# Retention's sample states handled four sequences at a time: column groups, 32-row pairs and 1 MB transfers

## The chip, the cores and the metric

The kernel runs on one core of a Trainium2 chip. The metric is the device time of one launch in microseconds; a change is judged by the median of several runs. Names of engines: TensorE (PE, and PEld for its weight loads), VectorE (DVE), ScalarE (ACT), GpSimd (POOL) and SyncE (SP). Transfers are issued by SyncE and GpSimd here and carried by 16 DMA engines.

## The reference, cut to what matters

One step of a hybrid encoder layer over 1024 prompt positions and 8 sample sequences of 16 positions each. The change touches the retention branch for the samples. Each of the 8 sequences has, for each of 4 heads, a state of 256 x 512 numbers that is read, used for the output and updated:

```python
def _retention_block(q, k, v, s, log_g):
    ...
    scores = jnp.einsum('bhnd,bhmd->bhnm', q, k) * decay
    out = jnp.einsum('bhnm,bhmv->bhnv', scores, v)
    q_dec = jnp.exp(lg * (idx + 1.0)).astype(dt)
    out = out + jnp.einsum('bhnd,bhdv->bhnv', q * q_dec[None, :, :, None], s)
    k_dec = jnp.exp(lg * (L - 1.0 - idx)).astype(dt)
    s_new = jnp.exp(log_g * L).astype(dt)[None, :, None, None] * s + jnp.einsum(
        'bhmd,bhmv->bhdv', k * k_dec[None, :, :, None], v)
    return out, s_new
```

The third-last einsum is called the state product below (q times the old state), the last one the update (k times v, added to the decayed state). Everything is in float32.

## The kernel before

Positions are cut into nine tiles of 128 (tile 0 holds the 8 x 16 sample positions, tiles 1 to 8 the prompt), and the tiles into three groups; group 0 is tiles 0 and 1. Each group goes through the trunk: `retention`, `gating`, `project`, `query`. After the trunk, or beside it, a product-key retrieval runs: its top-k work, gathered expert rows (GpSimd issues the gathers), and a long dense stage at the end.

Weights come in units of 512 KB, loaded by SyncE's queue up to 13 units ahead in group 0 (`load`, `take`). Each unit is split into two float32r parts, a high one on ScalarE (`whi`, L200) and a low one on VectorE (`wlo`, L204), and a product is made of three matmuls (`products`). The weight products are L176 (`gemm_f`) and L192 (`gemm_t`).

Only group 0 has sample states. For each head `retention` makes q, k and v, then `score`, then for tile 0 the loop over 8 sequences `b` and 2 halves `c` of the 256 state rows, 16 steps a head, 64 in all. This is called the state stretch of a head; it stands between the matmul of L383, with which tile 0's output `po` begins, and the two of L406 for tile 1. A step loads a state half of 128 x 512 (`load_state`, L292, 256 KB, ten buffers, four steps ahead), masks k to the 16 rows of sequence `b` and splits it (`kb`, L202 on ScalarE and L206 on VectorE), multiplies the masked `kb` with `vs` in three 128-row float32r matmuls (L395, the update), multiplies `qm` with the old state in float32 (L397, the state product; it writes 32 rows of `po`, which is one group of 32 columns of the array, given by `r = 2 * LS * (b // 2)`), adds the update on VectorE (L398) and stores the state half (L399, from GpSimd's queue). `qm` holds q of sequence `b` in 32 columns of which 16 are zero, so two sequences (`b` even and odd) add into the same 32 rows.

PSUM tiles named `sps` have four buffers, shared by `po`, the updates `pu` and the scores. A fp32 matmul has two records on TensorE, a float32r matmul one.

A scheduler sets the order of the instructions on every engine from the order in the code, priorities and its own costs; so weight products of the next gemm (L192) stand between the steps. On each engine the order is fixed at run time.

Of the kernel before, what the change touches and what calls it, by code (L numbers as in the profile page):

```python
# [8 lines left out]
F32 = mybir.dt.float32  # L9
# [5 lines left out]
OP = mybir.AluOpType  # L15
AX = mybir.AxisListType

P = 128
# [3 lines left out]
HEADS, DK, DV = 4, 256, 512  # L22
PH, NKEYS, TOPK = 8, 128, 16
HK = PH * TOPK
NB, LS = 8, 16
PAST = 512
EPS = 1e-6
GAMMA = [1.0 - 2.0 ** (-5.0 - h) for h in range(HEADS)]
# [7 lines left out]
K_KDP, K_EPP, K_DMP, K_TRI, K_IOTA, K_ID = 0, 4, 8, 520, 648, 776  # L36
N_CST = 904

S_KDS, S_EPS, S_DMS, S_TRS = 0, 32, 36, 548
N_SMP = 676  # L40

GROUPS = [[0, 1], [2, 3, 4, 5], [6, 7, 8]]

# [11 lines left out]
def step_kernel(ctx: ExitStack, tc: tile.TileContext, x, state, wall, wst, bs, rows, vec, cst, smp, cosd, sind, euv,  # L55
                eud, evd,
                y_p, y_s, st_p, st_s, sgu_s):
    nc = tc.nc
# [7 lines left out]
    sp = trunk_ps.enter_context(tc.tile_pool(name="sp", bufs=4, space=bass.MemoryType.PSUM))  # L66
# [76 lines left out]
    def products(w, a):  # L143
        return [(w[0], a[0]), (w[1], a[0]), (w[0], a[1])]
# [126 lines left out]
                yield from query(gi, pl, tl, nt, T, tT, rs, unit)  # L271
                flush(True)

    NSB, SBA = 10, 4

    def retention(pl, tl, nt, T, sample, hT, pb):
        cosT = pl.tile([P, T], F32, name="cosT")
# [2 lines left out]
        nc.sync.dma_start(sinT, sind[:, tl[0] * P:tl[0] * P + T])  # L280
        cos2 = cosT[:, None, :].to_broadcast([P, 2, T])
        sin2 = sinT[:, None, :].to_broadcast([P, 2, T])
        if sample:
            cm = pl.tile([P, S_TRS], F32, name="cm")
            nc.sync.dma_start(cm, smp[:, :S_TRS])
            Sbs = {}

            def load_state(n):
                for m in range(n if n > SBA - 1 else 0, min(n + 1, HEADS * NB * 2)):
                    Sbs[m] = pl.tile([P, DV], F32, name="Sb", bufs=NSB)  # L290
                    j, c = divmod(m, 2)
                    nc.sync.dma_start(Sbs[m], state[j % NB, j // NB, c * P:(c + 1) * P])  # L292

            load_state(SBA - 1)
            qm = pl.tile([P, 2, NB, 2 * LS], F32, name="qm")
            nc.vector.memset(qm, 0.0)

# [37 lines left out]
        for h in range(HEADS):  # L335
# [3 lines left out]
            q = rotary(ps, "q")  # L339
# [37 lines left out]
            for i, t in enumerate(tl):  # L377
# [4 lines left out]
                if t == 0:  # L382
                    mm(po, sc, v[:, i], start=True, stop=False)  # L383
                    vs = [pl.tile([P, DV], F32R, name=f"vs{j}") for j in range(2)]
                    split(vs, v[:, i])
                    for b in range(NB):
                        c0 = S_KDS + h * NB + b
                        for c in range(2):
                            load_state(2 * (h * NB + b) + c + SBA)
                            Sb = Sbs.pop(2 * (h * NB + b) + c)  # L390
                            kb = [pl.tile([P, P], F32R, name=f"kb{j}", bufs=2) for j in range(2)]
                            split(kb, kt[:, c * P:(c + 1) * P], cm[:, c0:c0 + 1])
                            pu = sp.tile([P, DV], F32, name="sps")
                            for j, (x, y) in enumerate(products(kb, vs)):
                                mm(pu, x, y, start=j == 0, stop=j == 2)  # L395
                            r = 2 * LS * (b // 2)
                            mm(po[r:r + 2 * LS], qm[:, c, b], Sb, start=False, stop=b % 2 == 1 and c == 1)  # L397
                            nc.vector.scalar_tensor_tensor(Sb, Sb, GAMMA[h] ** LS, pu, op0=OP.mult, op1=OP.add)  # L398
                            nc.gpsimd.dma_start(st_s[b, h, c * P:(c + 1) * P], Sb)  # L399
                        yield 3.5  # L400
                else:
                    mm(po, sc, v[:, i], start=True, stop=S is None)
                    pus = []
# [652 lines left out]
def constants():  # L1056
# [6 lines left out]
    for h in range(HEADS):  # L1063
        g = GAMMA[h]
        c[:, K_KDP + h] = g ** (P - 1 - m) / 16
        c[:, K_EPP + h] = EPS / g ** (2 * (m + 1))
        c[:, K_DMP + h * P:K_DMP + (h + 1) * P] = np.where(tri, g ** (-(m[:, None] + 1)) / 16, 0)
        for b in range(NB):
            d[:, S_KDS + h * NB + b] = np.where(m // LS == b, g ** (LS - 1 - m % LS) / 16, 0)
        d[:, S_EPS + h] = EPS / g ** (2 * (m % LS + 1))  # L1070
        d[:, S_DMS + h * P:S_DMS + (h + 1) * P] = np.where(tri & same, g ** (-(m[:, None] % LS + 1)) / 16, 0)
    c[:, K_TRI:K_TRI + P] = tri
# [55 lines left out]
```

## Time and profile before

| | before |
|---|---|
| median of 3 runs (lowest to highest) | 3954.83 us (3950.23 to 3957.91) |
| the profiled execution's own time | 3949.41 us |
| its span in the profile | 3947.5 us |
| TensorE busy, share of the span | 92% |
| VectorE, ScalarE, GpSimd | 87%, 47%, 26% |
| mean rate of HBM traffic over the span | 297 GB/s |

The span is the time from the first to the last instruction in the trace; the launch's own time has 1.9 us around it. Busy times are shares of the whole span, so an engine with a high share can still be idle in the stretch that a change touches. TensorE's matmuls are pipelined and the ends of their records are modelled: what a matmul costs is read from the distance between starts, which the pieces of the chain of waits give, not from the length of a record.

### The profile page before, as it was taken

How to read it: one execution, taken by the hardware profiler on the slowest of the kernel's cores; microseconds unless marked ns; L12 is line 12 of the kernel's file. 1: busy time of each engine (PE TensorE's matmuls, PEld its weight loads, DVE VectorE, ACT ScalarE, POOL GpSimd, SP SyncE). 2: the span in 40 equal slices, each digit the busy share in tenths (PEclk: the TensorE clock that was granted, in tenths of full speed). 3: DMA queues.
4: the chain of work that ended last, by engine and by line, in shares of the span. 5: the costliest groups of instructions: out<-in, count | busy, mean ns of one | idle time of the engine just before them, and what ended most of it. 6: DMA issues, size and time to landing. Idle time of an engine off the chain costs nothing.

```text
span 3947.5 us, 54950 instructions
## 1 busy us (share of the span) xinstructions
PE 3636.9 (92%) x19724; PEld 3085.6 (78%) x19724; DVE 3450.0 (87%) x6439; ACT 1847.1 (47%) x3879; POOL 1022.0 (26%) x740
## 2 busy tenths in 40 slices
PE   8999999999999898889889846999899999999998
PEld 6769988788788777778889845777777777777776
DVE  5555699999989799889898888999899999999996
ACT  4435544444343443765656737334334344443443
POOL 0010002333334230121212221234223333333330
PEclk9999999999999899999999967999999999999999
DMA  8665637999989893685777884899779999999994
GB/s 292 216 211 190 206 117 281 358 353 345 352 330 364 344 332 119 212 288 197 264 264 278 308 302 134 343 382 379 287 289 375 381 362 388 369 388 372 377 382 187
DMA packets 245298, 1176.03 MB, mean 298 GB/s; under 512 B 28193, under 2 KB 45345, under 8 KB 161057
## 3 DMA queue, kind: packets, MB, share of 16 engines
q0 software_dynamic: 105984, 721.47, 49.0%
q1 hardware_dynamic: 139040, 451.06, 31.2%
q8 instruction: 155, 2.54, 0.3%
q14 instruction: 119, 0.97, 0.1%
HBM read 1095.87 MB, written 76.55 MB: 297 GB/s over the span
## 4 chain that ended last, share of the span: by engine, by line
issue 34%; PE 19%; POOL 16%; DVE 16%; DMA 11%; ACT 3%; POOLq 0%; SPq 0%; DVEq 0%; ACTq 0%
POOL gat L778 16%; PE gps L176 6%; DMA pdr<-st 4%; PE gps L192 4%; DMA gat<-in_euv_dram,idx 3%; DVE acc L749 2%; PE S L1001 2%; DVE wlo L204 2%; DVE gat L739 2%; PE res L972 2%; PE sps L397 1%; PE sps L395 1%; DMA s<-ssp 1%; ACT st L806 1%; DVE ktmp L633 1%
## 5 line engine op out<-in xcount | busy, mean ns | idle before, releaser
L778 POOL DMA_INDIRECT gat<-in_euv_dram,idx x640 | 948.2, 1482 | 2378.8 <-DVE acc L749 1639.5
L739 DVE CUSTOM_DVE_ANT_0 gat<-gat,tx 128x1024 f32<-128x1024 f32 x640 | 782.6, 1223 | 68.7 <-DMA gat<-in_euv_dram,idx 52.7
L749 DVE SCALAR_TENSOR_TENSOR acc<-gat,sdot,acc 128x1024 f32<-128x1024 f32 x640 | 821.4, 1283 | 1.3 <-ACT sdot L745 0.9
L972 PE MATMUL res<-ev,g 128*128 128x512 f32 x2304 | 802.4, 393 | 8.8 <-ACT g L200 8.6
L1001 PE MATMUL S<-h,whi 128*128 128x512 f32 x2048 | 758.8, 398 | 10.0 <-ACT a L1006 5.9
L192 PE MATMUL gps<-whi,h 128*128 128x256 f32 x3456 | 661.2, 290 | 5.8 <-DVE rot L302 2.2
L204 DVE TENSOR_TENSOR wlo<-wraw,whi 128x1024 fp32r<-128x1024 f32 x428 | 523.7, 1224 | 82.1 <-ACT whi L200 80.7
L192 PEld LDWEIGHTS gps<-whi,h 128*128 128x128 f32 x3456 | 556.4, 196 | 29.5 <-issue 22.2
L200 ACT CAST whi<-wraw 128x1024 fp32r<-128x1024 f32 x428 | 447.3, 1045 | 260.6 <-PE gps L176 143.2
L744 ACT ACTIVATE sdot<-sdot 128x1 f32<-128x1 f32 x640 | 128.3, 202 | 839.4 <-DVE sdot L739 837.8
L972 PEld LDWEIGHTS res<-ev,g 128*128 128x128 f32 x2304 | 433.2, 189 | 111.5 <-ACT g L200 17.9
L192 PE MATMUL gps<-wlo,h 128*128 128x256 f32 x1728 | 500.8, 290 | 19.7 <-DVE wlo L204 19.7
L176 PE MATMUL gps<-h,whi 128*128 128x256 f32 (+2 forms) x1920 | 499.4, 343 | 10.5 <-ACT pb L328 5.8
L1001 PEld LDWEIGHTS S<-h,whi 128*128 128x128 f32 x2048 | 388.2, 190 | 118.6 <-ACT a L1006 33.3
L176 PE MATMUL gps<-y,whi 128*128 128x256 f32 (+2 forms) x1536 | 404.7, 346 | 21.1 <-ACT y L202 9.1
L1001 PE MATMUL S<-h,wlo 128*128 128x512 f32 x1024 | 402.0, 393 | 0.0
L176 PEld LDWEIGHTS gps<-h,whi 128*128 128x128 f32 x1920 | 345.0, 193 | 37.0 <-ACT pb L328 6.0
L192 PEld LDWEIGHTS gps<-wlo,h 128*128 128x128 f32 x1728 | 338.3, 196 | 34.0 <-DVE wlo L204 21.4
L176 PE MATMUL gps<-h,wlo 128*128 128x256 f32 (+2 forms) x960 | 328.5, 342 | 7.8 <-DVE wlo L204 7.7
L176 PEld LDWEIGHTS gps<-y,whi 128*128 128x128 f32 x1536 | 276.1, 193 | 47.3 <-ACT y L202 9.8
L200 ACT CAST ev<-wraw 128x512 fp32r<-128x512 f32 x256 | 158.1, 622 | 260.5 <-PE res L972 129.1
L176 PE MATMUL gps<-y,wlo 128*128 128x256 f32 (+2 forms) x768 | 263.1, 343 | 2.2 <-DVE wlo L204 2.2
(216 smaller groups left out, 5297.1 us busy)
## 6 DMA issues: line engine op xcount, KB each, us to landing
wraw<-in_wall_dram SPq DMA_DIRECT2D x300, 512.0 KB
wraw<-in_eud_dram SPq DMA_DIRECT2D x128, 512.0 KB
wraw<-in_evd_dram SPq DMA_DIRECT2D x128, 512.0 KB
gat<-in_wall_dram SPq DMA_DIRECT2D x84, 512.0 KB
pdr<-st POOLq DMA_DIRECT2D x32, 1024.0 KB
pt<-pdr SPq DMA_DIRECT2D x16, 2048.0 KB
Sb<-in_state_dram SPq DMA_DIRECT2D x64, 256.0 KB
out_dram<-Sb POOLq DMA_DIRECT2D x64, 256.0 KB
```

The source lines that it names most:

```text
L176: mm(ps[:, c, :T], x, y, start=kh == 0 and k == 0 and j == 0, stop=kh == nk - 1 and k == 3 and j == len(pr) - 1)
L192: mm(ps[:, i], y, x, start=kh == 0 and k == 0 and j == 0 and i % 2 == 0, stop=kh == 1 and k == 3 and j == len(pr) - 1 and last)
L200: nc.scalar.copy(parts[0], src)
L204: nc.vector.tensor_tensor(parts[1], src, parts[0].bitcast(F32), op=OP.subtract)
L395: mm(pu, x, y, start=j == 0, stop=j == 2)
L397: mm(po[r:r + 2 * LS], qm[:, c, b], Sb, start=False, stop=b % 2 == 1 and c == 1)
L739: nc.vector.tensor_tensor_reduce(out=b[:, :D], in0=b[:, :D], in1=d["x"], op0=OP.mult, op1=OP.add, scale=1.0, scalar=0.0, accum_out=d["s"][ ...
L744: nc.scalar.activation(d["s"][:, j:j + 1], d["s"][:, j:j + 1], AF.Gelu_apprx_tanh)
L749: nc.vector.scalar_tensor_tensor(d["acc"], b[:, D:], d["s"][:, j:j + 1], d["acc"], op0=OP.mult, op1=OP.add)
L778: nc.gpsimd.indirect_dma_start(out=b, out_offset=None, in_=euv, in_offset=bass.IndirectOffsetOnAxis(ap=d["idx"][:, j:j + 1], axis=0))
L972: mm(ps, x, y, start=start and i == 0, stop=stop and i == 2)
L1001: mm(ps, x, y, start=k == 0 and i == 0, stop=k == KD - 1 and i == 2)
```

## The change

Four sequences of the same parity (`a` is 0 or 1, `q` is 0 to 3, `b = 2 * q + a`) are taken together, so a head has four steps `(a, c)` instead of 16.

- One load of 1 MB brings the state halves of four sequences (`four`, L294, three buffers, one step ahead in the code); one store takes them back (L412).
- k is masked and split once a step: the mask now keeps every second block of 16 rows, so that each block of 32 rows holds one sequence of the step.
- The state products of the four sequences stand one after another in the code; they write four different groups of 32 rows of `po` (L400).
- The updates (L406) multiply only the 32 rows of a sequence, and two sequences take turns in each of the three matmuls of a product: rows 0 to 31 and 32 to 63, then 64 to 95 and 96 to 127. `keep_in_program_order` holds that order, except for the first matmul of a pair.
- VectorE still adds each update to its state by itself (L410). The yields sum to the same, 28 a head.

```diff
-S_KDS, S_EPS, S_DMS, S_TRS = 0, 32, 36, 548
-N_SMP = 676
+S_KDS, S_EPS, S_DMS, S_TRS = 0, 8, 12, 524
+N_SMP = 652
...
-    NSB, SBA = 10, 4
...
+        def four(z, h, a, c):
+            return z.rearrange("(q a) h k v -> a h k q v", a=2)[a, h, c * P:(c + 1) * P]
+
...
             def load_state(n):
-                for m in range(n if n > SBA - 1 else 0, min(n + 1, HEADS * NB * 2)):
-                    Sbs[m] = pl.tile([P, DV], F32, name="Sb", bufs=NSB)
-                    j, c = divmod(m, 2)
-                    nc.sync.dma_start(Sbs[m], state[j % NB, j // NB, c * P:(c + 1) * P])
-
-            load_state(SBA - 1)
+                if n < HEADS * 4:
+                    h, a, c = n // 4, n // 2 % 2, n % 2
+                    Sbs[n] = pl.tile([P, 4, DV], F32, name="Sb", bufs=3)
+                    nc.sync.dma_start(Sbs[n], four(state, h, a, c))
+
+            load_state(0)
...
-                    for b in range(NB):
-                        c0 = S_KDS + h * NB + b
+
+
+                    for a in range(2):
+                        c0 = S_KDS + h * 2 + a
                         for c in range(2):
-                            load_state(2 * (h * NB + b) + c + SBA)
-                            Sb = Sbs.pop(2 * (h * NB + b) + c)
+                            n = (h * 2 + a) * 2 + c
+                            load_state(n + 1)
+                            Sq = Sbs.pop(n)
                             kb = [pl.tile([P, P], F32R, name=f"kb{j}", bufs=2) for j in range(2)]
                             split(kb, kt[:, c * P:(c + 1) * P], cm[:, c0:c0 + 1])
-                            pu = sp.tile([P, DV], F32, name="sps")
-                            for j, (x, y) in enumerate(products(kb, vs)):
-                                mm(pu, x, y, start=j == 0, stop=j == 2)
-                            r = 2 * LS * (b // 2)
-                            mm(po[r:r + 2 * LS], qm[:, c, b], Sb, start=False, stop=b % 2 == 1 and c == 1)
-                            nc.vector.scalar_tensor_tensor(Sb, Sb, GAMMA[h] ** LS, pu, op0=OP.mult, op1=OP.add)
-                            nc.gpsimd.dma_start(st_s[b, h, c * P:(c + 1) * P], Sb)
-                        yield 3.5
+                            for q in range(4):
+                                r = slice(2 * LS * q, 2 * LS * (q + 1))
+                                mm(po[r], qm[:, c, 2 * q + a], Sq[:, q], start=False, stop=a == 1 and c == 1)
+                            for qs in ((0, 1), (2, 3)):
+                                pu = {q: sp.tile([P, DV], F32, name="sps") for q in qs}
+                                for j, (x, y) in enumerate(products(kb, vs)):
+                                    for q in qs:
+                                        r = slice(2 * LS * q, 2 * LS * (q + 1))
+                                        ins = mm(pu[q], x[r], y[r], start=j == 0, stop=j == 2)
+                                        if (j, q) != (0, qs[0]):
+                                            tc.keep_in_program_order(ins)
+                                for q in qs:
+                                    nc.vector.scalar_tensor_tensor(Sq[:, q], Sq[:, q], GAMMA[h] ** LS, pu[q],
+                                                                   op0=OP.mult, op1=OP.add)
+                            nc.gpsimd.dma_start(four(st_s, h, a, c), Sq)
+                            yield 7.0
...
-        for b in range(NB):
-            d[:, S_KDS + h * NB + b] = np.where(m // LS == b, g ** (LS - 1 - m % LS) / 16, 0)
+        for b in range(2):
+            d[:, S_KDS + h * 2 + b] = np.where(m // LS % 2 == b, g ** (LS - 1 - m % LS) / 16, 0)
```

TensorE's order before, in head 1's state stretch: from the sixth state product (L397) on, with updates (L395) and weight products (L192) between. A trailing x4 is four such instructions in a row.

```order
L397 MATMUL sps<-Sb,qm 32x512
L395 MATMUL sps<-vs_1169,kb_1253 128x512
L397 MATMUL sps<-Sb,qm 32x512 x4
L192 MATMUL gps<-whi,h_133 128x256
L395 MATMUL sps<-vs_1169,kb_1254 128x512
L395 MATMUL sps<-vs_1170,kb_1253 128x512
L395 MATMUL sps<-vs_1169,kb_1266 128x512
L397 MATMUL sps<-Sb,qm 32x512
L192 MATMUL gps<-wlo,h_133 128x256
L192 MATMUL gps<-whi,h_134 128x256
L192 MATMUL gps<-whi,h_133 128x256
```

Here the products mostly stand alone between updates, with one row of four.

TensorE's order in the changed kernel at the start of the same stretch, from its first matmul on (L385 is the former L383, L400 the products, L406 the updates).

```order
L385 MATMUL sps<-v,sc 128x512
L400 MATMUL sps<-Sb,qm 32x512 x4
L406 MATMUL sps<-vs_1079,kb_1085 128x512 x3
L406 MATMUL sps<-vs_1079,kb_1086 128x512 x2
L406 MATMUL sps<-vs_1080,kb_1085 128x512 x2
L400 MATMUL sps<-Sb,qm 32x512
L406 MATMUL sps<-vs_1079,kb_1085 128x512
L406 MATMUL sps<-vs_1079,kb_1086 128x512 x2
L406 MATMUL sps<-vs_1080,kb_1085 128x512 x2
L400 MATMUL sps<-Sb,qm 32x512 x3
L406 MATMUL sps<-vs_1079,kb_1116 128x512
L400 MATMUL sps<-Sb,qm 32x512
```

The products have moved together: the first step's four stand in a row, the second step's are one and three, the third step's too, and the last step's are four again further down. The updates of a pair take turns.

SyncE's queue in the changed kernel, from head 1's state stretch on: state loads (L294), weight loads (L124) and a store of the prompt's state (L157).

```order
L294 DMA Sb<-in_state_dram 128x4x512 x2
L124 DMA wraw<-in_wall_dram 128x1024
L294 DMA Sb<-in_state_dram 128x4x512
L157 DMA stsp_114<-S 128x1024
L294 DMA Sb<-in_state_dram 128x4x512
L124 DMA gat<-in_wall_dram 128x1024 x2
```

Thirteen, one and two loads of 256 KB stood in these places before; now it is two, one and one of 1 MB, of which the first is for the last step of head 1 and the other three for head 2.

From the gating stage of group 0 to the end of the program the order on every engine is the same in both kernels, and 48 loads, 48 stores and 48 pairs of mask-and-split are fewer ahead of it.

## Rows read from the trace of the kernel before

**Rows 1.** The page: the span, and busy time of each engine.

```profile
span 3947.5 us, 54950 instructions
...
PE 3636.9 (92%) x19724; PEld 3085.6 (78%) x19724; DVE 3450.0 (87%) x6439; ACT 1847.1 (47%) x3879; POOL 1022.0 (26%) x740
```

**Rows 2.** Windows by stretch: heads 0 to 3's state stretches and what lies between.

```profile
core 0: us, PE busy (x) PEld busy (x) DVE busy (x) ACT busy (x) POOL busy (x), PEclk, DMA share, GB/s
43.16:78.52 35.36, 35.36 (x107) 13.74 (x106) 18.12 (x37) 9.09 (x24) 8.89 (x16) 1.00 0.88 299
...
113.34:148.37 35.03, 35.03 (x122) 15.86 (x122) 18.61 (x38) 11.20 (x26) 8.52 (x16) 1.00 0.67 226
148.37:192.58 44.21, 44.21 (x374) 44.19 (x373) 25.41 (x35) 23.12 (x30) 0.12 (x1) 1.00 0.62 206
192.58:227.61 35.03, 35.03 (x122) 15.85 (x122) 18.61 (x38) 11.20 (x26) 8.53 (x16) 1.00 0.71 234
...
271.82:306.85 35.03, 35.03 (x123) 15.85 (x122) 18.62 (x38) 11.21 (x26) 8.52 (x16) 1.00 0.51 174
```

**Rows 3.** Chain of waits, head 1's state stretch: start us, us, what.

```profile
by line: PE sps L397 38.7%; PE sps L395 36.6%; PE gps L192 14.7%; PE sps L406 4.9%; PE sps L383 2.6%; PE sps L402 2.4%
...
113.34 0.91 PE sps L383 x2
...
124.33 0.97 PE sps L397 x2
...
125.73 1.85 PE sps L397 x8
...
131.87 0.93 PE sps L395 x4
...
145.28 0.86 PE sps L402 x2
...
146.65 1.72 PE sps L406 x4
```

**Rows 4.** Chain of waits, a run of weight products ahead of head 1's stretch.

```profile
100.49 11.52 PE gps L192 x96
```

**Rows 5.** Timeline of TensorE's weight loads: a lone product, then the row of four.

```profile
59.72 0.14 PEld L397 LDWEIGHTS sps<-Sb,qm 128*32 128x32 f32 x2 [0.36 <-issue]
...
125.66 0.15 PEld L397 LDWEIGHTS sps<-Sb,qm 128*32 128x32 f32 x4 [0.24 <-issue]
126.11 0.12 PEld L397 LDWEIGHTS sps<-Sb,qm 128*32 128x32 f32 x2 [0.31 <-issue]
126.54 0.12 PEld L397 LDWEIGHTS sps<-Sb,qm 128*32 128x32 f32 x2 [0.31 <-issue]
127.50 0.19 PEld L192 LDWEIGHTS gps<-whi,h 128*128 128x128 f32 x1 [0.84 <-issue]
```

**Rows 6.** Groups by line in head 1's stretch: busy us, mean ns | idle before.

```profile
L398 DVE SCALAR_TENSOR_TENSOR Sb<-Sb,sps 128x512 f32<-128x512 f32 x16 | 10.6, 685 | 16.1 <-PE sps L395 13.8 <-PE sps L397 2.3
...
L395 PEld LDWEIGHTS sps<-vs,kb 128*128 128x128 f32 x48 | 8.3, 188 | 7.1 <-ACT kb L202 4.0 <-DVE kb L206 2.3
L202 ACT ACTIVATE kb<-kt,cm 128x128 fp32r<-128x128 f32 x16 | 6.3, 401 | 17.2 <-PE sps L395 16.5 <-DVE Sb L398 0.6
...
L206 DVE SCALAR_TENSOR_TENSOR kb<-kt,cm,kb 128x128 fp32r<-128x128 f32 x16 | 5.1, 346 | 0.2 <-ACT kb L202 0.2
...
L397 PEld LDWEIGHTS sps<-Sb,qm 128*32 128x32 f32 x32 | 2.0, 108 | 4.8 <-issue 4.6
```

**Rows 7.** Timelines of GpSimd's stores and SyncE's queue, heads 0 and 1.

```profile
118.31 0.54 POOL L399 DMA_DIRECT2D out_dram<-Sb  x1 [39.95 <-DVE kb L206]
...
40.73 28.57 SPq L292 DMA_DIRECT2D Sb<-in_state_dram  x16
...
120.65 26.89 SPq L292 DMA_DIRECT2D Sb<-in_state_dram  x13
```

**Rows 8.** GpSimd's issue of a 1 MB store, later stage: ns min/median/max.

```profile
L808 POOL DMA_DIRECT2D pdr<-st x32: 1152/1213/1317, 1583.8 to 2455.7; - x32
```

## Prediction

> **What bounds the kernel now.** I began with the page: a span of 3947.5 us with TensorE at 92% [rows 1], and no other engine above VectorE's 87%. That share is a mean over stages, so I cut the stage of the change, group 0's retention, into stretches: in every one of them TensorE is busy from end to end at a granted clock of 1.00 (2.4 GHz), while VectorE has work for about half of a state stretch, ScalarE for a third and GpSimd for a quarter [rows 2]. So TensorE's queue sets the length here, and a microsecond taken off ScalarE, VectorE or an issuing queue alone is worth nothing.
>
> Next the chain of waits through head 1's state stretch, 113.34 to 148.37 us. All of its pieces are TensorE's: 38.7% products (L397) and 36.6% updates (L395) [rows 3]. Heads 2 and 3 show the same busy times [rows 2]. After it the chain stays on TensorE's weight products, and the order of instructions on every engine is the same in both programs from the gating stage on; so what retention saves moves everything behind it forward, one for one.
>
> **Prices on TensorE.** A full-width weight product takes 11.52 / 96 = 0.12 us [rows 4]. An update takes 0.93 / 4 = 0.23; a lone state product 0.97 (two records of one fp32 matmul); L383, L402 and the two of L406 take 0.91, 0.86 and 1.72, so 3.49 together [rows 3]. The 35.03 us of the stretch are then 3.49, 32 weight products (3.8), 48 updates (11.0), and 16.7 for 16 products: twelve lone ones at 0.97 and one row of four, which took 1.85 [rows 3], are 13.5. The 3.2 left over I put down to changing the array's shape: 13 times in and out, 0.125 a change. One shows at 127.50: the weight loader stood idle for 0.84 before it took the next full-width weights, where otherwise it runs ahead [rows 5].
>
> **The row of four** is what decides. It holds the seventh to tenth product of the head (b = 3, 3, 4, 4), so its products 1 and 2 write column group 1, products 3 and 4 group 2. Their first weight loads, four of them, all begin inside 0.15 us at 125.66, and two further pairs follow at 126.11 and 126.54 [rows 5]: one product of either group ran beside one of the other, so four took 1.85 where lone ones take 3.9. TensorE reached past product 2 to start product 3. In the new program four in a row have four different groups.
>
> **The sum, heads 1 to 3.** Unchanged: 3.49. The new order puts 39 weight products inside the stretch, 32 before: 4.7 (and 0.84 fewer behind it, so the old stretch on this footing is 35.9). The 16 products stand in six rows (4, 1, 3, 1, 3, 4). All groups of a row at once is 6 x 0.97 = 5.8; two at once, 4 x 1.85 + 2 x 0.97 = 9.3. I take 5.8, since the second group cost nothing that the rows show; 9.3 stays as a bound. The 48 updates are as many as before, but on 32 rows each, in pairs on two row groups and two PSUM tiles. No row of this kernel has a 32-row matmul. Below: 24 x 0.23 = 5.5, side by side as the column groups were. Above: one after another, 11.0; with the weight load of 0.188 [rows 6] no longer hidden, 20.1. I take 5.5, as the nearest rows show two groups of the array truly side by side [rows 5]. Changes of shape: the new order has 22, 2.75. Sum 22.3. Then waits: a pair needs two of the three PSUM tiles that the output leaves free, so it waits for an update of 0.69 on VectorE [rows 6]; the weight products set between the pairs cover most of that. I add 1.5 for this and the loads: 23.8. Saved: 35.9 - 23.8 = 12.1 a head.
>
> **Head 0.** 35.36 before [rows 2] with 16 weight products; the new order has 55, so 40.0 on the same footing. New: 3.49 + 6.6 + four rows of four at 0.97 (3.9) + 5.5 + 21 changes (2.6) = 22.1, and 2.5 for waits, since its loads after the first are issued only from about 41 us on, behind weights [rows 7]: 24.6. Saved: 15.4. Together 15.4 + 3 x 12.1 = 52; I forecast 51.
>
> **What I cost at nothing.** 48 of 64 mask-and-split pairs go: 48 x 0.40 on ScalarE and 48 x 0.35 on VectorE [rows 6], 36 us of work under a TensorE that is never idle. Of VectorE's 18.6 us in a stretch [rows 2] 12 splits go, and 14.5 stay beside TensorE's 24. SyncE issues 16 loads instead of 64; GpSimd issues 4 stores a head in place of 16, and a 1 MB store elsewhere in the kernel costs it 1.21 [rows 8], with nothing else to do there. If TensorE's cover were gone, VectorE would hold a head at 14.5 and no lower.
>
> **Loads.** Three tiles of 1 MB, so step 3's load waits for step 0's store. Before, a 256 KB store issued at 118.31 freed its tile for the load at 120.65, 2.34 us later [rows 7]. The DMA engines moved 299 GB/s at 88% busy [rows 2], about 340 when full, so 0.79 MB more is 2.3: 4.6 for the store, and as much for the load. Step 0's updates end some 7 us into the stretch (0.91, two rows of products, twelve updates in pairs, five changes, two sums of 0.69 and the 0.6 or so that GpSimd starts behind them); 7 + 4.6 + 4.6 = 16.2. TensorE wants the tile where 16.4 of the 22.3 are done. That is just in time, and contention is in the 1.5. SyncE's queue holds weight loads behind these waiting loads, as before: in head 1 it issued 13 state loads over 26.89 us [rows 7], and no TensorE wait followed, since up to 13 units are fetched ahead. Head 1 moves 226 GB/s x 35.0 + 206 x 44.2 = 17 MB [rows 2]; in 67 us instead of 79 that is 254 GB/s, below 340.
>
> **Where the skill bears.** The Trainium skill, page "TensorE: Matmul & The Clock Gate", section Part 3, says that weight loads overlap running matmuls only where the row group differs, which would deny it to column groups. This case's trace differs: at 126.11 two loads of 0.12 begin while both groups stream [rows 5]. The same page measured four 32-row tiles at 3.07 times one; an estimate from that (77% efficiency, so 1.53 for a pair) makes the updates 7.2 instead of 5.5 a head and the saving 45 in all; no run here shows it yet.
>
> **The rivals.** Updates do not pair (13%): 11.0 for 5.5, and VectorE's wait vanishes under them: 36 saved, 3919.
>
> Products go two at once (10%): 9.3 for 5.8, and 7.4 for 3.9 in head 0: 38 saved, 3917. With unpaired updates too (6%): 31.3 and 31.2 a head, 23 saved, 3932.
>
> Weight loads are laid bare within a row (4%): 32 loads of 0.108 [rows 6], 3.5 a head, 14 less: 3918. The overlap at 126.11 speaks against it. This is where the Trainium skill's rule (TensorE: Matmul & The Clock Gate, Part 3) would lead.
>
> The load of step 3 comes late (6%): if a 1 MB turn takes four of the old 2.07 (26.89 / 13), 8.3 each way, it lands at 24 instead of 16.2: 7 a head, 28 less, 3932. Against it: those turns were paced by the updates, not by the engines.
>
> Nothing (4%): if a 32-row update costs 0.40, the 48 of them eat what the products give.
>
> Slower (5%): each 32-row update is its own change of shape, with load bare: 0.23 + 0.19 + 0.125 = 0.54, 26.1 a head. Then 42.8 stands against 35.9 (and 42.7 against 40.0): 23 us slower, 3978. It decides from 0.40 on. Speaking for it: no row shows what a new row group costs; against it: a second column group cost next to nothing, as its two loads fit with the first two into 0.15 us, where those of a lone product take 0.14 [rows 5].
>
> **How the numbers follow.** The profiled execution took 3949.4, 5.4 below the median of 3954.8 that is to be predicted; from the median, 3954.8 - 51 = 3904. That case has 52%. Without any wait the saving is 17.9 + 3 x 13.6 = 59, so 3896, and the runs differ by some 4: low 3892. The high end takes in both half-gains together: 3935. A measurement of this kernel tells 0.2%, 8 us, from no change: faster 0.91, same 0.04, slower 0.05.
>
> **What will show it.** Right: rows of L400 with eight matmul records in about 1.0 us instead of 1.85; pairs of L406 that start within 0.02 us of each other; state stretches of 22 to 25 us from L385 to the last L419; everything from the gating stage on shifted by one amount. Wrong: L406 at 0.23 or more apart within a pair; a wait of TensorE on a load at the last L400 row of a head; TensorE waiting for VectorE's L410 for more than 2 us a head; or a granted clock below 1.00 in the stretches.

## The result, and the profile after

The changed kernel took 3911.4 us (median of 4 runs, 3908.6 to 3916.1) against 3954.9 us for the kernel before on the same chip: a ratio of 0.9892, 95% interval 0.9875 to 0.9909, or 43 us off. The forecast was 3904, with a range of 3892 to 3935. The profiled execution took 3911.4 us.

The page, in the lines that answer to [rows 1]:

```profile
span 3909.7 us, 54608 instructions
...
PE 3583.4 (92%) x19724; PEld 3060.1 (78%) x19724; DVE 3433.9 (88%) x6391; ACT 1838.5 (47%) x3839; POOL 986.5 (25%) x692
```

TensorE's share is the same 92% of a shorter span. ScalarE and VectorE shed some work, and the whole says nothing of where the 43 us lie. The windows by stretch do, beside [rows 2]. The first group below is the four state stretches and one gap between them; the second cuts head 0 finely.

```profile
core 0: us, PE busy (x) PEld busy (x) DVE busy (x) ACT busy (x) POOL busy (x), PEclk, DMA share, GB/s
43.49:75.88 32.39, 29.04 (x147) 15.67 (x146) 16.91 (x28) 9.59 (x17) 3.26 (x4) 0.79 0.98 338
105.86:129.51 23.65, 23.57 (x131) 12.07 (x130) 15.29 (x26) 6.77 (x14) 3.01 (x4) 1.00 0.69 243
129.51:173.03 43.52, 43.48 (x367) 43.26 (x365) 25.39 (x35) 25.42 (x32) 0.00 (x0) 1.00 0.72 258
173.03:197.04 24.01, 23.63 (x131) 12.06 (x130) 15.29 (x26) 6.77 (x14) 3.01 (x4) 1.00 0.76 251
240.13:263.81 23.68, 23.60 (x131) 12.06 (x130) 15.29 (x26) 6.77 (x14) 3.01 (x4) 1.00 0.65 229
...
44.00:50.00 6.00, 5.91 (x39) 3.16 (x37) 5.11 (x9) 2.05 (x6) 0.00 (x0) 1.00 1.02 372
50.00:58.00 8.00, 8.00 (x64) 5.27 (x60) 3.97 (x6) 2.62 (x3) 1.18 (x2) 1.00 0.98 362
60.00:62.00 2.00, 1.75 (x10) 1.01 (x9) 1.10 (x2) 1.34 (x2) 0.61 (x1) 1.00 1.02 264
62.00:64.00 2.00, 0.00 (x0) 0.00 (x0) 0.00 (x0) 0.19 (x1) 0.14 (x1) 0.52 0.95 321
64.00:66.00 2.00, 1.10 (x8) 0.20 (x8) 0.00 (x0) 0.00 (x0) 0.00 (x0) 0.50 1.03 422
74.00:76.00 2.00, 2.00 (x6) 0.96 (x5) 1.33 (x4) 0.08 (x1) 0.00 (x0) 0.57 1.04 418
76.00:78.00 2.00, 2.00 (x20) 2.00 (x19) 1.11 (x3) 1.45 (x5) 0.00 (x0) 1.00 1.03 412
```

Heads 1 to 3 take 23.65, 24.01 and 23.68 us where 23.8 was forecast. Head 0 takes 32.39 where 24.6 was forecast: TensorE stands for 3.15 us (the window 62 to 64 of the second group has no work of it at all), and from 62 to 75.7 us the granted clock is 0.50, the lower level (1.2 GHz; 0.57 in the window 74 to 76 puts its end there).

The chain of waits through head 1's stretch (start us, us, what), as in [rows 3]:

```profile
115.86 0.89 PE sps L406 x6
116.74 0.67 PE gps L192 x4
...
123.34 1.00 PE sps L400 x8
```

A row of four state products (L400, eight records; q times the old state, which is the second-last einsum of the reference and not the third-last) takes 1.00 us; before, a row of four that had only two column groups took 1.85 and a lone one 0.97. Six updates on 32 rows (three pairs, L406) take 0.89. The same chain in head 0:

```profile
50.35 7.50 DMA out_dram<-Sb
...
57.87 6.98 DMA Sb<-in_state_dram
...
64.90 1.94 PE sps L400 x8
66.84 0.72 PE sps L406
67.56 1.37 PE gps L192 x5
```

The store of step 0 takes 7.50 us, the load of step 3 behind it 6.98, and only then does TensorE go on, at half speed: 1.94 for a row that takes 1.00 elsewhere. In the rows that answer to [rows 6, 7], an update's sum on VectorE (L410) is 0.68 long, as before, and a store of 1 MB costs GpSimd 0.75 to start, where one of 256 KB cost 0.54 and where [rows 8] had 1.21.

Two measures are used below, since from the gating stage on the same instructions took between 3554 and 3585 us in the profiles, which is as much as some of the effects. One is the **period** of a head, from its first product of scores and values (L385) to that of the next head; the other is the start of the first matmul of the gating stage, 391.09 before and 346.57 after. The changed kernel profiled a second time gave 346.29.

| kernel | period, head 0 | heads 1, 2 | us in products, head 1 | gating starts | ratio to before (95%) |
|---|---|---|---|---|---|
| before | 70.17 | 79.24, 79.25 | 13.56 | 391.09 | 1 |
| changed | 62.37 | 67.17, 67.10 | 5.92 | 346.57 | 0.9892 (0.9875 to 0.9909) |
| spare tiles, head 0 | 55.51 | 67.22, 66.79 | 5.92 | 339.31 | 0.9861 (0.9841 to 0.9881) |
| small transfers | 60.21 | 68.85, 68.99 | 8.11 | 349.54 | 0.9893 (0.9874 to 0.9913) |
| one row group | 64.83 | 74.50, 77.97 | 5.92 | 377.60 | 0.9968 (0.9953 to 0.9983) |
| full rows | 57.10 | 70.05, 70.08 | 5.92 | 350.05 | 0.9918 (0.9897 to 0.9940) |
| sequence by sequence | 65.25 | 70.27, 74.47 | 4.95 | 364.37 | 0.9900 (0.9870 to 0.9929) |
| one column group | 72.45 | 76.31, 75.62 | 11.89 | 385.13 | 0.9966 (0.9951 to 0.9982) |
| transfers only | 66.84 | 72.71, 72.71 | 7.86 | 369.43 | 0.9909 (0.9881 to 0.9936) |
| order alone | 67.45 | 77.47, 77.47 | 11.74 | 384.30 | 0.9978 (0.9967 to 0.9989) |
| whole rows | 54.65 | 72.89, 70.81 | 4.85 | 352.78 | 0.9878 (0.9856 to 0.9899) |
| whole rows, all spare | 54.71 | 64.18, 64.17 | 3.98 | 330.17 | 0.9853 (0.9838 to 0.9868) |

### The profile page after: what moved, and what is told of

It is laid out like the page before. It is cut to its first block, busy times and chain, and to the rows that moved or that the text cites. A ratio compares the mean times of both kernels' runs of the same rounds, so it can differ in the third digit from the quotient of the medians.

```text
span 3909.7 us, 54608 instructions
## 1 busy us (share of the span) xinstructions
PE 3583.4 (92%) x19724; PEld 3060.1 (78%) x19724; DVE 3433.9 (88%) x6391; ACT 1838.5 (47%) x3839; POOL 986.5 (25%) x692
## 4 chain that ended last, share of the span: by engine, by line
issue 33%; PE 19%; DVE 17%; POOL 15%; DMA 12%; ACT 4%; POOLq 0%; SPq 0%; DVEq 0%; ACTq 0%
POOL gat L791 15%; PE gps L176 6%; DMA pdr<-st 4%; PE S L1014 4%; PE gps L192 3%; DMA gat<-in_euv_dram,idx 3%; DVE wlo L204 3%; DVE acc L762 2%; PE res L985 2%; DVE gat L752 2%; PE blk L985 1%; DMA s<-ssp 1%; DVE ktmp L646 1%; ACT whi L200 1%; ACT st L819 1%
## 5 line engine op out<-in xcount | busy, mean ns | idle before, releaser
L791 POOL DMA_INDIRECT gat<-in_euv_dram,idx x640 | 935.4, 1462 | 2395.9 <-DVE acc L762 1651.9
L192 PE MATMUL gps<-whi,h 128*128 128x256 f32 x3456 | 660.4, 290 | 5.2 <-ACT whi L200 1.9
L192 PEld LDWEIGHTS gps<-whi,h 128*128 128x128 f32 x3456 | 556.2, 196 | 18.4 <-issue 11.8
L192 PE MATMUL gps<-wlo,h 128*128 128x256 f32 x1728 | 500.9, 290 | 20.7 <-DVE wlo L204 20.7
L192 PEld LDWEIGHTS gps<-wlo,h 128*128 128x128 f32 x1728 | 338.4, 196 | 30.1 <-DVE wlo L204 22.4
L176 PEld LDWEIGHTS gps<-y,whi 128*128 128x128 f32 x1536 | 272.6, 191 | 47.5 <-ACT y L202 10.8
```

What stands on the lines that cost most here:

```text
L176: mm(ps[:, c, :T], x, y, start=kh == 0 and k == 0 and j == 0, stop=kh == nk - 1 and k == 3 and j == len(pr) - 1)
L192: mm(ps[:, i], y, x, start=kh == 0 and k == 0 and j == 0 and i % 2 == 0, stop=kh == 1 and k == 3 and j == len(pr) - 1 and last)
L791: nc.gpsimd.indirect_dma_start(out=b, out_offset=None, in_=euv, in_offset=bass.IndirectOffsetOnAxis(ap=d["idx"][:, j:j + 1], axis=0))
```

## The experiments

### What head 0 lost: spare tiles, small transfers

Head 0's step 3 was given two tiles of 512 KB that another pool has idle there, so that its load waits for no store:

```diff
+                    if n == 3:
+                        two = [peer.tile([P, D], F32, name="acc", bufs=2).rearrange("p (q v) -> p q v", v=DV)
+                               for _ in range(2)]
+                        for j in range(2):
+                            nc.sync.dma_start(two[j], four(state, h, a, c)[:, 2 * j:2 * j + 2])
+                        Sbs[n] = [two[q // 2][:, q % 2] for q in range(4)], two
+                        return
...
```

> Head 0's step 3 gets two 512 KB tiles that are idle at that point, so its load waits for no store; nothing else changes. Theory (head 0 lost its gain to the wait of the fourth load on the first store, 3.15 us of TensorE waiting, and to the lower clock behind it, 0.50 to 0.52 from 65 to 76 us, some 5 us more): no wait of TensorE on the state tile in head 0, a granted clock of 1.00 right through, head 0's stretch 24 to 25 us instead of 32.4, and about 8 us off the whole, 3903. Rival (the DMA engines are full from 44 to 58 us whatever the load waits for, so it only queues elsewhere): stretch 31 to 33, time 3911.

3898.0 us, ratio 0.9861. Windows of this kernel: the whole of head 0's stretch, then the 4 us in which the changed kernel stopped.

```profile
43.40:66.59 23.19, 22.91 (x135) 12.05 (x134) 14.80 (x26) 5.48 (x13) 3.46 (x5) 1.00 1.01 351
60.00:62.00 2.00, 2.00 (x8) 0.46 (x7) 1.18 (x2) 0.08 (x1) 0.53 (x1) 1.00 1.01 365
62.00:64.00 2.00, 2.00 (x15) 1.22 (x14) 0.53 (x2) 1.40 (x4) 0.23 (x1) 1.00 0.99 311
```

The stretch is 23.19 us, the clock 1.00 throughout, although the DMA engines are as full (1.01) as they were. Head 0's period falls by 6.9 us and the gating starts 7.3 us sooner. So the theory stands: the wait for a tile and what followed on the clock took head 0's gain, not the fullness of the engines by itself. The intervals of the two ratios overlap; it is the windows and the gating's start that tell this kernel from the changed one.

The other way to free a tile sooner is to cut the transfers again, four of 256 KB for each step, in the same memory:

```diff
-                    Sbs[n] = pl.tile([P, 4, DV], F32, name="Sb", bufs=3)
-                    nc.sync.dma_start(Sbs[n], four(state, h, a, c))
+                    Sbs[n] = [pl.tile([P, DV], F32, name="Sb", bufs=12) for _ in range(4)]
+                    for q in range(4):
+                        nc.sync.dma_start(Sbs[n][q], four(state, h, a, c)[:, q])
...
```

> Each step's state in four tiles of 256 KB with a load and a store each (12 buffers, the same memory), all else as in the changed kernel. Theory (a store of the whole step frees the tile too late): the first store of head 0 can start after the first pair's sums, some 3 us sooner, so most of the 3.15 us wait goes and with it the fall of the clock: head 0's stretch 25 to 28, time 3904 to 3907. Rival (the DMA engines are full there anyway, and 64 loads and 64 stores need more turns): head 0's stretch stays at 32 and the other heads lose 0 to 1 us each: 3911 to 3915.

3908.0 us, ratio 0.9893: no difference from the changed kernel. Neither case came out whole. Head 0 has no wait above 0.6 us and a clock of 1.00, and its period is 2.2 us shorter; heads 1 and 2 are 1.7 to 1.9 us longer. The reason is in the products: with states arriving one by one the order that comes out has eight rows in head 1 (4, 1, 3, 1, 3, 1, 2, 1) instead of six, 8.11 us instead of 5.92.

### What a pair of updates costs: one row group, full rows, sequence by sequence

```diff
-                                        r = slice(2 * LS * q, 2 * LS * (q + 1))
+                                        r = slice(0, 2 * LS)
                                         ins = mm(pu[q], x[r], y[r], start=j == 0, stop=j == 2)
```

> Every update reads rows 0 to 31 of the array (so each uses the first sequence's tokens, which changes the state that is written); number, size and order of the matmuls stay. Theory (the pairs run side by side because their row groups differ): 24 pairs at 0.46 instead of 0.23, 5.5 us a head in heads 1 to 3 and as much or less in head 0: 3911 + 17 to 22 = 3928 to 3933. Rival (updates of 32 rows are short, or lie beside the weight products, for another reason, and the row group does not matter): within 3 us of 3911. A third reading (weight loads of the same rows cannot overlap either): 0.18 more for each of 48, 8.7 a head more, 3960 or above.

3939.9 us, ratio 0.9968: 28 us more by the medians, 31 by the gating's start. Chain of waits, head 1, and windows at the end of head 0's stretch:

```profile
116.28 1.58 PE sps L406 x6
...
62.00:64.00 2.00, 2.00 (x10) 1.33 (x9) 1.29 (x2) 0.50 (x2) 0.00 (x0) 0.97 0.91 265
64.00:66.00 2.00, 2.00 (x9) 1.12 (x11) 0.00 (x0) 1.03 (x2) 0.75 (x1) 0.50 1.02 414
```

Six updates take 1.58 instead of 0.89, which is 0.23 for each pair, and 24 x 0.23 is the 5.5 us a head of the theory. The rest goes with the clock: it falls to 0.50 near the end of the stretches, in head 0 at 63.9 us, with TensorE busy without a gap. That part none of the readings had.

```diff
-                                        ins = mm(pu[q], x[r], y[r], start=j == 0, stop=j == 2)
+                                        ins = mm(pu[q], x, y, start=j == 0, stop=j == 2)
```

> Every update reads all 128 rows (so each adds up the four sequences of its step, which changes the state that is written); number and order stay. Theory (a pair costs one update because of its two row groups, and a change into and out of a 32-row shape costs 0.125 us as put into the forecast): updates +5.5 us a head, about ten changes of shape less, -1.2: +4.2 a head, 3911 + 17 = 3928, and below the kernel with all updates on rows 0 to 31 by some 4 us. Rival (a change of row shape costs nothing): the same as that kernel, 3931 to 3933. Rival (32-row updates are not side by side and gain nothing): 3906 to 3911.

3921.6 us, ratio 0.9918; periods of heads 1 and 2 are 70.05 and 70.08, 2.9 us above the changed kernel's, where the theory had 4.2. Chain of waits:

```profile
113.77 1.50 PE sps L406 x6
115.27 0.47 PE gps L192 x4
```

A run of six costs 0.6 more than in pairs, but the four weight products behind it cost 0.47 instead of 0.67: each passage from 32 rows to 128 and back is paid for, 0.2 a time. A change of row shape therefore has a price (that rival falls), near the 0.25 put in for a passage (two changes of 0.125) and not above it. What was put in too high is the gain of pairs: taken from their start to that of the next matmul, the 48 updates of head 1 come to 8.1 us in pairs and 12.3 here, 4.2 apart and not 5.5, and the 39 weight products of the stretch give 0.8 of it back. That is 3.4 in the stretch, and 2.9 by the period. In head 0 TensorE waited only 0.5 us for the late load, the slower updates having filled the time; the clock stayed at 1.00, and the period is 57.10.

```diff
-                                for j, (x, y) in enumerate(products(kb, vs)):
-                                    for q in qs:
+                                for q in qs:
+                                    for j, (x, y) in enumerate(products(kb, vs)):
```

> The updates of a pair are written one product after the other (three matmuls on rows 0 to 31, then three on rows 32 to 63) instead of taking turns; same matmuls, output unchanged. Theory (TensorE lets a matmul run beside another only where it stands next to it or one further): two of six meet a neighbour of the other row group, five slots of 0.23 for three, and the third of a sequence meets the first of the next: nine slots for twelve updates instead of six, +0.7 a step, +2.8 a head: 3918 to 3923. Rival (it reaches past any number of matmuls): 3909 to 3913. Rival (nothing pairs without the alternation): +5.5 a head, with a fall of the clock as in the kernel with all updates on one row group: 3931 to 3940.

3921.6 us, ratio 0.9900, which by itself does not tell it from the changed kernel; the gating starts 17.8 us later. The timeline of TensorE, then of its weight loads:

```profile
116.66 0.98 PE L406 MATMUL sps<-vs,kb 32*128 32x512 f32 x9
118.39 0.96 PE L406 MATMUL sps<-vs,kb 32*128 32x512 f32 x3 [0.76 <-DVE Sb L410]
...
116.65 0.55 PEld L406 LDWEIGHTS sps<-vs,kb 32*128 32x128 f32 x9 [0.84 <-ACT kb L202]
```

No expectation comes out whole. The time lies in the theory's range, but not for its reason; the mechanism is that of the first rival, whose time it misses. Nine matmuls, three sequences written one after the other (by the code; the rows do not name the row groups), are done in 0.98 us, hardly more than a lone sequence's three (0.96): TensorE reaches past the matmuls of the same rows and runs three row groups side by side. The alternation in the program is not what makes the pairs. What is lost is the wait for VectorE: three tiles of PSUM fill at once, the fourth sequence stands until a sum frees one (0.5 to 0.8 us, 6.7 us over the four heads), and the weight products, which the order no longer puts in between, do not cover it. Loads that come late (8.8 us in all) and the lower clock behind them go with the rest.

### What a row of products costs: one column group, transfers only, order alone

```diff
+                                last = a == 1 and c == 1
-                                r = slice(2 * LS * q, 2 * LS * (q + 1))
+                                r = slice(2 * LS * q, 2 * LS * (q + 1)) if last else slice(0, 2 * LS)
...
```

> The products of steps 0 to 2 of every head all write rows 0 to 31 of the sum (so the output of three quarters of the sample products lands in the wrong rows); step 3 keeps its four groups. Theory (four products cost one because their column groups differ): the twelve products of steps 0 to 2 cost 0.97 each instead of five rows of 0.99, +6.7 us in heads 1 to 3; in head 0 +8.7, of which the 3.15 us wait and the 5 us of lower clock of the changed kernel may be absorbed, since the store of step 0 gains time: 21 to 29 us, 3932 to 3940. Rival (a row of four is cheap because the four loads of weights come together, whatever the group): 3909 to 3913. If the clock falls at the end of the stretches, as with the updates on one row group, 3 to 5 us more a head.

3948.0 us, ratio 0.9966: 37 us more by the medians, 29 by the ratios. Timeline, head 1:

```profile
117.24 3.62 PE L401 MATMUL sps<-Sb,qm 128*32 128x512 f32 x8
...
136.04 1.06 PE L401 MATMUL sps<-Sb,qm 128*32 128x512 f32 x8 [1.64 <-DMA Sb<-in_state_dram]
```

Four products on one group take 3.62, four on four groups (the second row) 1.06 (from their start to that of the next matmul, 3.55 and 1.00): the theory stands for the products. It had thought that head 0's wait might be absorbed. It was not: here it is 5.9 us, the longest of four that come to 11.4, and the clock is down behind it.

The 1 MB transfers without the rest (per sequence its own mask, its 128-row update and its product, in the new order of steps):

```diff
...
+                            for q in range(4):
+                                kb = [pl.tile([P, P], F32R, name=f"kb{j}", bufs=2) for j in range(2)]
+                                c0 = S_KDS + h * NB + 2 * q + a
+                                split(kb, kt[:, c * P:(c + 1) * P], cm[:, c0:c0 + 1])
+                                pu = sp.tile([P, DV], F32, name="sps")
+                                for j, (x, y) in enumerate(products(kb, vs)):
+                                    mm(pu, x, y, start=j == 0, stop=j == 2)
+                                r = slice(2 * LS * q, 2 * LS * (q + 1))
+                                mm(po[r], qm[:, c, 2 * q + a], Sq[:, q], start=False, stop=a == 1 and c == 1)
...
```

> The 1 MB transfers alone: states in tiles of four sequences, one load and one store for four, three tiles; products, masks and updates for each sequence apart, on 128 rows, as before the change. Theory (the gain is all TensorE's; transfers and the 48 masks and splits are off its path): 3950 to 3960, no change against before. Rival (fewer transfers give part of the gain): 3935 to 3945. Rival (a load that waits for the store of a whole step costs every head): 3965 to 3985.

3930.9 us (3922.8 to 3955.9), ratio 0.9909; the gating starts at 369.43, 21.7 us sooner than before. The theory is refuted as it was put. But it is not the transfers' own time that went, since TensorE waited for no state in either kernel. The timeline shows products of neighbouring sequences running together, two in 1.05, three in 1.06 (from start to next start 0.98 and 0.99):

```profile
113.63 1.05 PE L403 MATMUL sps<-Sb,qm 128*32 128x512 f32 x4
...
117.15 1.06 PE L403 MATMUL sps<-Sb,qm 128*32 128x512 f32 x6
```

Products fall from 13.56 to 7.86 us a head and the period by 6.5. To part the order of sequences from the transfers, the kernel before was run with nothing changed but that order:

```diff
-                    for b in range(NB):
+                    for k in range(16):
+                        a, c, b = k // 8, k // 4 % 2, 2 * (k % 4) + k // 8
...
```

> The kernel before with nothing changed but the order in which the sixteen updates and products of a head are written: even sequences first, then odd ones, both halves of a sequence apart, so that neighbouring products write different column groups; transfers of 256 KB, masks and 128-row updates stay. Theory (what the kernel with the 1 MB transfers alone gained, gating at 369.4 against 391.1, came from this order, not from the transfers): gating starts at 368 to 372, some 20 us off the whole, ratio 0.994 to 0.996. Rival (the transfers gave it): gating at 388 to 392, no change. In between, both have a part.

3944.8 us, ratio 0.9978, gating at 384.30: in between. Products take 11.74 us a head, 1.82 less than before, and the period is 1.77 less. So writing neighbours into different column groups gives under a third; the rest came with the 1 MB transfers, by way of the order: with four states arriving together, a head has three rows of three products and two of two, where the order alone has one of three and two of two. Why the instructions come out in that order was not tried further.

### What the lower clock follows: full rows and two tiles

Updates on all 128 rows as above, and `bufs=2` for the states' tiles.

> Updates on all 128 rows (each adds up the four sequences of its step, which changes the state that is written) and two tiles for the states instead of three, so that loads wait for the store of the step before and TensorE waits for them. It tells what the lower clock follows. Reading A (a wait of TensorE of about 3 us or more is enough): behind every such wait in the stretches the granted clock is 0.50 for several us. Reading B (it takes 32-row updates ahead of the wait, as it fell without any wait where all updates ran on rows 0 to 31 one after another): 1.00 behind waits of 3 us. If the weight products that the order puts ahead of the waiting products cover the loads, there is no wait over 1 us and it tells nothing.

One run, 3929.4 us, too little to compare times by. TensorE waits for states five times, 16.6 us in all. Windows around the longest wait, which begins at 129.4:

```profile
128.00:130.00 2.00, 1.42 (x8) 0.90 (x6) 1.50 (x3) 1.05 (x1) 0.70 (x1) 1.00 0.20 41
130.00:132.00 2.00, 0.00 (x0) 0.00 (x0) 0.72 (x1) 0.00 (x0) 0.05 (x1) 1.00 0.94 310
132.00:134.00 2.00, 0.00 (x0) 0.00 (x0) 0.00 (x0) 0.00 (x0) 0.00 (x0) 0.62 1.05 378
134.00:136.00 2.00, 1.64 (x8) 0.20 (x8) 0.00 (x0) 0.00 (x0) 0.00 (x0) 0.50 1.02 418
```

The clock is 1.00 through the first 3 us of this wait of 4.94 us and 0.50 after that, and it is the same in the wait of 4.84. Of the two waits of 2.7 us, the clock fell behind one, over a microsecond after TensorE had gone on, and not behind the other; behind the one of 1.41 it did not fall. So the fall needs no 32-row updates ahead of it: reading B falls. Reading A fits these waits, but not the run with all updates on one row group, in which the clock fell without a wait; what the lower clock follows is left open.

Nor can the work ahead be read from how soon the clock falls. In the changed kernel it was down some 0.3 us after TensorE stopped at 61.75. In its second profile, the same program, TensorE stopped at 61.77 and the clock held for 3.1 us more:

```profile
62.00:64.00 2.00, 0.00 (x0) 0.00 (x0) 0.00 (x0) 0.21 (x1) 0.16 (x1) 1.00 1.06 298
64.00:66.00 2.00, 0.00 (x0) 0.00 (x0) 0.00 (x0) 0.00 (x0) 0.00 (x0) 0.71 1.02 347
```

Spare tiles, with the same 32-row pairs and no wait, kept 1.00.

### A kernel that beats both: whole rows, spare tiles in every head

The table points to fewer rows of products. Held in program order, each step's four products stay one row:

```diff
-                                mm(po[r], qm[:, c, 2 * q + a], Sq[q], start=False, stop=a == 1 and c == 1)
+                                ins = mm(po[r], qm[:, c, 2 * q + a], Sq[q], start=False, stop=a == 1 and c == 1)
+                                tc.keep_in_program_order(ins)
```

> As the kernel with the two spare tiles, and in addition the four products of a step are held in program order, so that every head has four rows of four (4, 4, 4, 4) instead of six rows (4, 1, 3, 1, 3, 4) in heads 1 to 3. Theory (a row costs 0.98 however many of the four groups it holds): two rows less, -2.0 us a head in heads 1 to 3, -6 in all: 3892 against 3898, and stretches of heads 1 to 3 that are 2 us shorter at the same number of weight products. Rival (a row costs by its products, and a lone one runs beside the updates around it): no change, 3898. Rival (a step that starts its products later frees its tile later, so a load comes late): one or more waits of TensorE on a state tile, 3898 to 3910.

3917.5 us, ratio 0.9878, gating at 352.78. The third reading came true, at a higher price than it had. Chain of waits, head 1:

```profile
109.54 8.09 DMA Sb<-in_state_dram
...
117.68 1.94 PE sps L408 x8
```

The last step wants its state sooner, the load behind the store of step 0 has not got sooner, TensorE waits 4.1 us and goes on at half speed. Spare tiles for step 3 of every head (`if n % 4 == 3` in place of `if n == 3`) take that away:

> The whole rows of the run before with spare tiles for step 3 of every head, not of head 0 alone, so no load within a head waits for the store of the same head's step 0. Theory (whole rows lost in heads 1 to 3 only to the late load, about 4 us each, and to the lower clock behind it): no wait over 1 us on a state tile, a granted clock of 1.00 in all four stretches, four rows of four at 1.00 in each head; gating starts 5 to 7 us sooner than in the kernel with the spare tiles of head 0 alone (339.3), at 333 to 335, and the time is about 18 us under the changed kernel's in the same runs. Rival (the DMA engines cannot bring 1 MB more in that time, whatever the tiles): waits of several us stay and the gating starts at 340 or later.

> The changed kernel itself, beside the others on the same chip, to have all three kernels side by side: ratio to the kernel before 0.987 to 0.991; gating starts at 346 to 347, head 0 with the lower clock behind its wait as in its first profile.

3896.8 us, ratio 0.9853 (0.9838 to 0.9868), beside 3911.9 and 0.9897 (0.9879 to 0.9914) for the changed kernel in the same runs: 15 us faster, and 57 faster than before. From spare tiles in head 0 alone (0.9841 to 0.9881) the times do not part it; the gating's start does. Head 1's stretch, by windows and chain:

```profile
98.01:115.85 17.84, 17.15 (x105) 7.79 (x103) 13.64 (x25) 5.72 (x13) 3.68 (x5) 1.00 0.68 223
...
106.75 1.00 PE sps L408 x8
107.75 0.95 PE sps L415 x6
108.69 0.69 DVE Sb L419
```

Four rows of 1.00 (in head 0 the fourth took 1.37), a clock of 1.00, no wait for a state over 1 us; the gating starts at 330.17, 3 us sooner than the theory had it and 9.1 us before that of spare tiles in head 0 alone, 3 a head. Two rows are 1.94 of it; the other microsecond goes with fewer passages between products and updates, which is argued, not shown. Now VectorE's sums stand in the chain, so a next gain may lie in PSUM tiles or in VectorE; that was not tried.

## Why the prediction was right, and where it was not

**Products.** The row that decided was read rightly: 13.5 forecast for the old products and 5.8 for the new, 13.56 and 5.92 measured. Both experiments on columns bear it out. The sentence in Part 3 of the Trainium skill, page "TensorE: Matmul & The Clock Gate", which lets weight loads overlap only where the row group differs, does not fit this case: eight records of four column groups are done in 1.00 us.

**Updates.** A pair does cost what one update of 32 rows costs, as forecast (three sequences side by side 0.98 and one alone 0.96; three pairs 0.89, and 1.58 where they share rows). But a run of three pairs is not 3 x 0.23, and pairing was worth only 2.9 us a head against 128-row updates, where 5.5 less 1.25 for ten more changes of shape would be 4.2. The estimate of 7.2 us a head, which goes by the 3.07 in Part 3 of the Trainium skill, page "TensorE: Matmul & The Clock Gate", is not settled by the totals: the runs of updates take 8.1 us in head 1, but with the passages into 32 rows in them. Side by side, three row groups show no such loss (0.98 against 0.96).

The saving of a head came out right, 12.1 forecast and 12.1 measured, and that is in part luck. Products gave 7.6, where 7.7 was forecast. Updates, changes of shape and waits stood in the sum at 5.5 + 2.75 + 1.5 = 9.75 and took 9.5 (23.65 less 3.49, 4.7 and 5.92), but not in these parts: TensorE stood idle for 0.08 us in head 1's stretch, so updates and changes took 1.2 more than forecast, and the 1.5 put in for waits made up for it. Full rows already saved 9.2 of the 12.1.

**Work costed at nothing.** ScalarE, VectorE and the queues were indeed hidden in heads 1 to 3. The transfers were not quite nothing: the order of products came with them, and the load of step 3 was in only just in time, as forecast. In head 1 it landed at 123.13, and the row that needs it began at 123.27; in head 2 TensorE stood 0.4 us. No run took the masks away alone.

**Head 0** is where the forecast failed: 15.4 saved was forecast, 7.8 measured. The step is "4.6 for the store, and as much for the load", with 2.5 for waits. Both numbers came from the mean of a whole stretch, 299 GB/s at 88% busy. In the stretch itself the engines were full, 1.02 from 44 to 50 and 0.98 from 50 to 58 us, with the loads and stores of steps 1 and 2 and units of weights under way; the store took 7.50 and the load 6.98, and TensorE stood 3.15. In head 1 the same store took 4.7 and the load 5.9, and the chain shows no such wait. Its windows, the store in the first and the load in the second, have shares of 0.46 and 0.90:

```profile
112.00:118.00 6.00, 6.00 (x37) 2.93 (x34) 3.14 (x7) 0.40 (x1) 0.75 (x1) 1.00 0.46 175
118.00:124.00 6.00, 6.00 (x45) 4.20 (x42) 2.69 (x6) 1.05 (x1) 1.51 (x2) 1.00 0.90 322
```

The windows that would have warned were there; those of the kernel before, from 44 to 50 us, read:

```profile
44.00:50.00 6.00, 6.00 (x18) 2.50 (x18) 3.83 (x9) 2.18 (x7) 1.32 (x2) 1.00 1.02 393
```

The rival "the load of step 3 comes late" so came true in one head of four. It priced the wait and not what follows: from 64.90 to 75.7 us TensorE ran at half speed (a row 1.94 instead of 1.00), so half of these 10.8 us, an estimated 5.4, was lost behind a wait of 3.15. The two come to 8.5; the spare tiles gave back 6.9, with a last row that came out as one and three and cost 1.8 more (5.76 us of products, not 3.98). Two signs of being wrong that the forecast had set itself, a wait at the last row of L400 and a clock below 1.00, thus showed in head 0. With spare tiles in head 0 the saving is 14.7 against the 15.4 forecast, and the gating starts 51.8 us sooner, against 51 forecast in all.

**Other rivals.** Updates that do not pair, products two at once, bare weight loads, nothing, and slower: the row of 1.00 and the run of 0.89 rule them out.

## What to carry to other kernels

Where a matmul uses only 32 rows or 32 columns of the array, count groups of neighbours on different strips, not matmuls: here a group of one to four products cost 1.0 us, and a group of one to three sequences of updates 0.9 to 1.0. Larger transfers hold a tile until the last byte is stored, so size the buffers by the fullness of the DMA engines in the very microseconds in which the tile must turn over, not by the mean of the stage. A wait of TensorE may cost more than itself: look at the granted clock behind it.

## What the runs showed that was not expected

- The granted clock fell to 0.50 with TensorE busy without a gap, near the end of a stretch whose updates ran one after another on 32 rows; with pairs and no wait it stayed at 1.00.
- How long it stays down differs, for one program too: in the changed kernel 13.7 us (62.1 to 75.7) around a wait of 3.15, and in its second profile 10.2 us (64.9 to 75.1) around a wait of 4.74; in the run with full rows and two tiles 3.4 us (74.4 to 77.8) behind a wait of 2.68.
- Nine matmuls of three sequences, written sequence by sequence, ran in 0.98 us, as long as the three of one.
- One passage from 32-row to 128-row matmuls and back cost 0.2 us.
